# Four of six parts of the modulation as float32 products on TensorE, in groups of 32 columns

## The chip, the cores and the metric

The kernel runs on one core of a Trainium2 chip, in one launch. The metric is the device time in microseconds, the median of several runs. The engines are PE (TensorE, matrix products), DVE (VectorE), ACT (ScalarE), POOL (GpSimd) and SP, whose queue issues the DMAs. Each engine takes its instructions strictly in the order in which they stand in its program.

## The reference

Two layers of a hybrid backbone over 1024 latent tokens of width 1024: a Conformer convolution module and a multi-scale pooling mixer. Each layer is modulated by three vectors of 1024 (shift, scale, gate), products of a vector `silu(c)` with a 1024x3072 matrix. With two layers these are the six parts of the modulation:

```
for i in range(DEPTH):                       # DEPTH = 2, kinds: convolution, pooling
    sh, sc, gt = split((silu(c) @ w_mod[i] + b_mod[i])[:, None, :], 3)
    h = _rms(x, norm_g[i]) * (1.0 + sc) + sh
    o = _conv_mixer(h, ...) if kind == MIX_CONV else _pool_mixer(h, ...)
    x = x + gt * o

def _conv_mixer(h, w_in, dw, db, ln_g, ln_b, w_out):
    a, b, g = split(h @ w_in, 3)
    y = a * sigmoid(b)
    y = depthwise_conv(y, dw, width=31) + db      # along the tokens
    y = silu(_layernorm(y, ln_g, ln_b)) * silu(g)
    return y @ w_out
```

## The kernel before

Channels lie on the 128 partitions in eight tiles (ct or kt from 0 to 7), tokens on the free axis in two halves h of 512. A big product is made of three float32r products (hi x hi, lo x hi, hi x lo) by `mm3` (L192), and the parts hi and lo come from ACT (L156) and from DVE or POOL (L161), for tokens and weights alike.

The order in the program: the first shift and scale (`mod_block`, L300) and `hT`; the first products `pf` for the first half (PSUM names of the products: `pf`, `pg`, `ps` give y, `psg` the gates g); then two parts of the modulation by `gemv` (L262: `gt0`, whose dots run on POOL and ACT, and `sh1` on DVE); the products `pg`; then for the tiles 4 to 7 the products `ps`, with a third part `a1` stepped in between (`step`, L78). Behind the tile 4 stand the convolutions of the tiles 0 to 4 of the first half, and behind each of the next tiles its own. A convolution has 31 taps and runs either on DVE, with accumulators `cv` in PSUM (L448), or on ACT and POOL: ACT scales the shifted tile by a tap into a tile `pr` (L435), and POOL adds it to `z` (L436). POOL has the tiles 1, 3 and 5 of the first half and 1, 3, 5, 6 and 7 of the second. The first layer norm sums the eight `z` (`zsum`, L493), takes the mean on PE (`mu`, L498), the variance (`va`, then `vpz` on PE and `vrz`, a power on POOL, L226) and spreads the result by `rbz` (L231). The gate products `psg` fill PE around it. The output product of the first half, layer 1 for the first half (`psv`, `psq`, `psy`, `psf`) and the convolutions of the second half then run side by side up to the second layer norm. The fourth part, `gt1`, is stepped through layer 1. Behind the second layer norm come the second half's output product and layer 1.

Buffers are rings dealt in the order of the program: `raw` (four buffers) holds raw weights and the rows of `w_mod`, `w` their split parts, `pr` (two buffers) the scaled taps, and the PSUM tag `mm` has five banks. What is dealt later in the program waits until the buffer's last user is done. A scheduler then sets each engine's order; `behind` (L174) and `priority` (L72) steer it.

Of the kernel before, what the change touches and what calls it, by code (L numbers as in the profile page):

```python
# [14 lines left out]
P = 128  # L15
# [42 lines left out]
def hybrid_kernel(ctx, tc, xT, vecs, wm, cv_first, cv_w, cv_wo, pl_w, pl_grp, pl_wo, out):  # L58
# [24 lines left out]
    def unit(tag, name, dt=F32, cols=1024):  # L83
        """A [128, 1024] tile in a ring, or in a slot of a region (a letter and a number)."""
        width = WIDTH.get(tag[0], 1024)
        return S.tile([P, width], dt, tag=tag, name=name, bufs=RINGS.get(tag, 1))[:, :cols]
# [4 lines left out]
    def raw(name):  # L91
        return unit("raw", name)
# [37 lines left out]
    # window / count of the positions whose window is cut by an end of the sequence  # L130
# [17 lines left out]
    nc.vector.tensor_tensor(out=s_c, in0=s_c, in1=VT[:, :, V_C], op=ALU.mult)  # L148
    bsc = const.tile([P, 2, KT], F32, name="bsc")
# [31 lines left out]
    def load_next(out, in_):  # L181
        ordered(nc.sync.dma_start(out=out, in_=in_))
# [17 lines left out]
    def gemm(ps, w, r, after=(), start=KT // 2):  # L200
        """The products from start on are issued behind the instructions given."""
        for kt in range(KT):
            with behind(after if kt >= start else ()):
                mm3(ps, cut(w, bl(kt)), r[kt], kt == 0, kt == KT - 1)

    def diagonals(dg, cols):
        """[128, 4, 128] of the four columns, each on the diagonal of a block."""
        return nc.vector.tensor_tensor(
            out=dg.rearrange("p (j q) -> p j q", j=4),
            in0=ident.unsqueeze(1).broadcast_to((P, 4, P)),  # L210
            in1=cols.unsqueeze(2).broadcast_to((P, 4, P)),
            op=ALU.mult,
        )
# [3 lines left out]
    def rstd_rows(total, name, fill=None):  # L217
        """[128, 512] of 1 / sqrt(sum over the partitions of the total / D + EPS), on every partition."""
# [19 lines left out]
    def squares(xs, name, eng):  # L238
        """A sum of squares over the tiles, which grows by a tile at every call of add."""
        total = half("vs", f"va{name}")  # L240

        def add(i):
            if i == 0:
                nc.scalar.activation(total, xs[i], AF.Square)
                return None
            sq = half("sq", f"sq{name}{i}")
            nc.scalar.activation(sq, xs[i], AF.Square)  # L247
            return eng.tensor_tensor(out=total, in0=total, in1=sq, op=ALU.add)  # L248

        return total, add  # L250

    def dot(w, out, eng):
        """The sum over the rows of w_mod of their product with silu(c), for 128 of the outputs."""
# [8 lines left out]
    def gemv(layer, part, res, eng, after=()):  # L262
        for kt in range(KT):
            w = raw(f"wm{layer}{part}{kt}")
            nc.sync.dma_start(out=w, in_=wm[layer, part, kt])
            with behind(after):
                dot(w, res[:, kt : kt + 1], eng)
            if kt < KT - 1:
                yield True
        add = bsc[:, layer, :] if part == 1 else VT[:, :, V_BM + 3 * layer + part]  # L270
        nc.vector.tensor_tensor(out=res, in0=res, in1=add, op=ALU.add)
        if part == 1:
            nc.vector.tensor_tensor(out=res, in0=res, in1=VT[:, :, V_G0 + layer], op=ALU.mult)

# [17 lines left out]
    s_row = const.tile([P, D], F32, name="s_row")  # L292
# [7 lines left out]
    def mod_block(kt):  # L300
        dots = []
        for part in range(2):
            w = unit("w" if part else "raw", f"wmb{kt}{part}")
            load_next(w, wm[0, part, kt])
# [82 lines left out]
    early = [gemv(0, 2, gt0, nc.gpsimd), gemv(1, 0, sh1, nc.vector)]  # L387
    for i in range(KT):
        with behind(gated if i >= DOTS_AHEAD else []):
            for job in early:  # L390
                next(job, None)
    pending.append(gemv(1, 1, a1, nc.vector))
# [18 lines left out]
    def conv(h, ct, taps=None, count=None):  # L411
        """The convolution of a tile of channels, or the next ones (count) of its taps."""
# [105 lines left out]
    def gate_norm(h, z, rb):  # L518
        """Normed, gated and split; the norm runs two tiles ahead of the rest."""
# [92 lines left out]
    def load_early(part, k):  # L612
        """One of the weights of the first products of layer 1."""
# [120 lines left out]
    def layer1_out(part, ms, ahead=(), last=None, after=(), start=KT // 2):  # L734
        """The output product: of the first ones (ahead, loaded early) a tile of channels per k, the others in turn."""
# [36 lines left out]
    pending.append(gemv(1, 2, gt1, nc.vector))  # L772
# [78 lines left out]
```

## Time and profile before

| | us |
|---|---|
| median of 3 runs | 812.97 |
| lowest, highest | 811.77, 813.42 |
| span of the profiled execution, first to last instruction | 810.0 |
| busy PE, DVE, POOL, ACT in that span | 703.4, 671.5, 566.9, 407.5 |

The runs are device times, the span is the part of one execution that the profiler saw; no other time of that execution is recorded, so what lies around the span is taken as the median less the span, 2.97 us. Matmuls are pipelined and the end of each is modelled, so their spacing, not their length, tells what one costs. An engine that is busy all the time isn't therefore the one on which the end depends; the chain of work and the stretches tell that.

### The profile page before, as it was taken

What the parts mean: (1) busy time and instruction counts of PE and PEld (TensorE: products, weight loads), DVE (VectorE), ACT (ScalarE), POOL (GpSimd) and SP (SyncE); (2) the same over time, 40 slices, a digit from 0 to 9 for tenths busy, and PEclk for the clock granted to TensorE, in tenths of its full rate; (3) what the DMA queues carried; (4) which work ended last, traced back from release to release, by engine and by line L of the source; (5) the groups of instructions that cost most, each with busy time, mean ns of one, the idle gap of its engine ahead of it and who ended that gap; (6) DMA issues with size and microseconds to landing.
All of it is one profiled execution on the core that took longest, in us unless ns stands there. A gap on an engine that the chain in (4) does not pass through costs nothing.

```text
span 810.0 us, 9060 instructions
## 1 busy us (share of the span) xinstructions
PE 703.4 (87%) x3092; PEld 562.2 (69%) x3092; DVE 671.5 (83%) x782; ACT 407.5 (50%) x591; POOL 566.9 (70%) x412
## 2 busy tenths in 40 slices
PE   2887899699999969789899776878799979999998
PEld 1565788488878747468677555656578758888998
DVE  6989999899889799999999899999895572666521
ACT  4543853665666766556766645554332432333210
POOL 3398589999999989789989999898411630444322
PEclk9988999899999989999899978989999989999999
DMA  8673555311012422434521233444642550233232
GB/s 316 239 283 107 189 185 196 104 52 53 27 52 91 168 106 91 144 129 162 179 102 40 78 132 134 137 156 155 233 156 103 158 168 0 91 104 131 79 106 80
DMA packets 36478, 105.63 MB, mean 130 GB/s; under 512 B 4048, under 2 KB 6224, under 8 KB 36432
## 3 DMA queue, kind: packets, MB, share of 16 engines
q1 hardware_dynamic: 36432, 105.05, 37.7%
q8 instruction: 24, 0.39, 0.2%
q14 instruction: 22, 0.18, 0.1%
HBM read 92.45 MB, written 12.58 MB: 130 GB/s over the span
## 4 chain that ended last, share of the span: by engine, by line
DVE 32%; PE 26%; POOL 23%; issue 12%; ACT 4%; DMA 2%; SPq 0%; POOLq 0%; DVEq 0%; ACTq 0%
POOL z L436 18%; DVE cv L448 5%; PE psv L195 2%; PE psv L193 2%; PE psv L194 2%; PE psf L194 2%; PE psf L193 2%; PE psf L195 2%; PE psq L195 2%; PE psq L193 2%; PE psq L194 2%; PE pso L193 2%; PE pso L195 2%; PE pso L194 2%; DVE s L644 2%
## 5 line engine op out<-in xcount | busy, mean ns | idle before, releaser
L436 POOL TENSOR_TENSOR z<-z,pr 128x512 f32<-128x512 f32 (+8 forms) x240 | 381.9, 1592 | 30.7 <-ACT pr L435 16.3
L435 ACT ACTIVATE pr<-y,VT 128x512 f32<-128x512 f32 (+8 forms) x240 | 171.1, 718 | 131.4 <-POOL z L436 128.2
L448 DVE SCALAR_TENSOR_TENSOR cv<-y,VT,cv 128x512 f32<-128x512 f32 (+12 forms) x232 | 160.2, 740 | 0.2
L255 DVE SCALAR_TENSOR_TENSOR wm<-wm,s_row 128x1024 f32<-128x1024 f32 x24 | 44.6, 1861 | 0.1
L640 DVE TENSOR_TENSOR s<-v 128x519 f32<-128x519 f32 (+1 forms) x16 | 21.4, 1341 | 19.5 <-ACT v L689 19.5
L742 DVE SCALAR_TENSOR_TENSOR xf<-psf,gt,xf 128x260 f32<-128x260 f32 (+1 forms) x24 | 13.2, 570 | 29.2 <-PE psf L195 25.2
L259 POOL TENSOR_TENSOR wmb<-wmb,s_row 128x1024 f32<-128x1024 f32 x8 | 22.2, 2772 | 18.2 <-DMA wmb<-in_wm 18.2
L725 DVE SCALAR_TENSOR_TENSOR q<-psy,VT,q 128x260 f32<-128x260 f32 (+1 forms) x24 | 13.5, 569 | 19.2 <-PE psy L195 19.1
L259 POOL TENSOR_TENSOR wm<-wm,s_row 128x1024 f32<-128x1024 f32 x8 | 20.4, 2556 | 12.2 <-DMA wm<-in_wm 12.2
L536 ACT ACTIVATE z<-z,VT 128x512 f32<-128x512 f32 x16 | 12.9, 814 | 27.9 <-DVE z L533 27.9
L644 DVE TENSOR_TENSOR s<-s 128x517 f32<-128x517 f32 (+5 forms) x24 | 22.8, 956 | 0.2
L248 DVE TENSOR_TENSOR vay<-vay,sqy 128x512 f32<-128x512 f32 x14 | 16.5, 1180 | 5.5 <-ACT sqy L247 5.3
L655 DVE SCALAR_TENSOR_TENSOR s<-s,v 128x504 f32<-128x504 f32 (+1 forms) x16 | 19.6, 1235 | 1.4 <-POOL s L653 1.3
L156 ACT CAST y<-q 128x504 fp32r<-128x504 f32 (+1 forms) x16 | 9.9, 616 | 19.7 <-DVE q L725 19.7
L161 DVE TENSOR_TENSOR y<-q,y 128x504 fp32r<-128x504 f32 (+1 forms) x16 | 16.6, 1041 | 3.0 <-ACT y L156 3.0
L161 POOL TENSOR_TENSOR wo16l<-wo,wo16h 128x1024 fp32r<-128x1024 f32 x1 | 2.4, 2393 | 23.5 <-ACT wo16h L156 23.5
L161 DVE TENSOR_TENSOR pd<-s,pd 128x504 fp32r<-128x504 f32 (+1 forms) x16 | 17.5, 1107 | 1.6 <-ACT pd L156 1.4
L255 DVE SCALAR_TENSOR_TENSOR wmb<-wmb,s_row 128x1024 f32<-128x1024 f32 x8 | 15.5, 1933 | 3.0 <-DMA wmb<-in_wm 3.0
L550 DVE SCALAR_TENSOR_TENSOR xr<-pso,gt,xr 128x512 f32<-128x512 f32 x16 | 11.6, 743 | 7.2 <-PE pso L195 7.2
L513 DVE TENSOR_TENSOR va<-va,sqz 128x512 f32<-128x512 f32 x14 | 16.8, 1203 | 0.7
L528 DVE TENSOR_TENSOR z<-z,sgr 128x512 f32<-128x512 f32 x16 | 16.2, 1010 | 1.1 <-ACT z L536 1.1
L156 ACT CAST pd<-s 128x504 fp32r<-128x504 f32 (+1 forms) x16 | 9.7, 617 | 14.5 <-DVE s L655 10.2
(2497 smaller groups left out, 2463.6 us busy)
## 6 DMA issues: line engine op xcount, KB each, us to landing
wm<-in_wm SPq DMA_DIRECT2D x32, 512.0 KB, 3.3
wmb<-in_wm SPq DMA_DIRECT2D x16, 512.0 KB, 6.0
wo<-in_cv_wo SPq DMA_DIRECT2D x16, 512.0 KB, 3.8
wp<-in_pl_wo SPq DMA_DIRECT2D x16, 512.0 KB, 3.2
wg<-in_cv_w SPq DMA_DIRECT2D x12, 512.0 KB, 3.3
wv<-in_pl_w SPq DMA_DIRECT2D x12, 512.0 KB, 3.4
wq<-in_pl_w SPq DMA_DIRECT2D x12, 512.0 KB, 3.3
x<-in_xT SPq DMA_DIRECT2D x16, 256.0 KB, 5.6
```

The lines of the kernel that those rows point to most:

```text
L156: return nc.scalar.copy(hi, src)
L161: return eng.tensor_tensor(out=lo, in0=src, in1=hi.bitcast(F32), op=ALU.subtract)
L193: nc.tensor.matmul(ps, w[0], r[0], start=first, stop=False)
L194: nc.tensor.matmul(ps, w[0], r[1], start=False, stop=False)
L195: nc.tensor.matmul(ps, w[1], r[0], start=False, stop=last)
L255: eng.scalar_tensor_tensor(out=w, in0=w, scalar=1.0, in1=s_row, op0=ALU.mult, op1=ALU.mult, accum_out=out)
L259: eng.tensor_tensor(out=w, in0=w, in1=s_row, op=ALU.mult)
L435: nc.scalar.activation(pr[:, o], y[:, i], AF.Copy, scale=dw(k))
L436: nc.gpsimd.tensor_tensor(out=z[:, o], in0=z[:, o], in1=pr[:, o], op=ALU.add)
L448: nc.vector.scalar_tensor_tensor(out=a[:, o], in0=y[:, i], scalar=dw(k), in1=a[:, o], op0=ALU.mult, op1=ALU.add)
L640: nc.vector.tensor_tensor(out=s[:, :m], in0=v[:, :m], in1=v[:, 1 : m + 1], op=ALU.add)
L644: nc.vector.tensor_tensor(out=s[:, :m], in0=s[:, :m], in1=s[:, step : step + m], op=ALU.add)
```

## The change

The parts `gt0`, `sh1`, `a1` and `gt1` are no longer dots of rows of `w_mod` with a spread `silu(c)` on DVE or POOL. Each half (512 outputs) of a part becomes eight float32 products on PE: the weights are `silu(c)` repeated in 32 columns (`srep`), the data are 512 columns of `w_mod`, and product kt goes to the 32 partitions of group kt mod 4 of one bank `gv`. ACT copies the bank to a tile `row` of the ring `pr`, and four one-column products with a vector `sel`, one at the first partition of each group, add the four groups and turn the row into columns. DVE adds the bias and, for `a1`, multiplies. The bytes loaded are the same, in the same 512 KB pieces through `raw`. The first shift and scale stay as dots. `s_row` moves into a slot of a region, and one `behind` waits for one instruction, not two.

```diff
+    srep = const.tile([P, KT, 32], F32, name="srep")
+    nc.vector.tensor_copy(srep, s_c.unsqueeze(2).broadcast_to((P, KT, 32)))
+    sel = const.tile([P, 1], F32, name="sel")
+    nc.gpsimd.memset(sel, 0.0)
+    for j in range(4):
+        nc.gpsimd.memset(sel[32 * j : 32 * j + 1, :], 1.0)
...
-    def gemv(layer, part, res, eng, after=()):
-        for kt in range(KT):
-            w = raw(f"wm{layer}{part}{kt}")
-            nc.sync.dma_start(out=w, in_=wm[layer, part, kt])
-            with behind(after):
-                dot(w, res[:, kt : kt + 1], eng)
-            if kt < KT - 1:
+    def gemv(job, layer, part, res):
+        for h in range(2):
+            ps = mmps(f"gv{job}{h}")
+            for c in range(4):
+                w = raw(f"wk{job}{h}{c}")
+                nc.sync.dma_start(out=w, in_=wk[job, h, c])
+                for i in range(2):
+                    kt = 2 * c + i
+                    q = slice(32 * (kt % 4), 32 * (kt % 4) + 32)
+                    nc.tensor.matmul(ps[q, :], srep[:, kt, :], w[:, hs(i)], start=kt < 4, stop=kt >= 4)
+                if c < 3:
+                    yield True
+            row = half("pr", f"row{job}{h}")
+            nc.scalar.copy(row[:, :HW], ps)
+            for j in range(4):
+                nc.tensor.matmul(ps[:, j : j + 1], row[:, bl(j)], sel, start=True, stop=True)
+            o = slice(4 * h, 4 * h + 4)
+            add = bsc[:, layer, o] if part == 1 else VT[:, o, V_BM + 3 * layer + part]
+            nc.vector.tensor_tensor(out=res[:, o], in0=ps[:, :4], in1=add, op=ALU.add)
+            if part == 1:
+                nc.vector.tensor_tensor(out=res[:, o], in0=res[:, o], in1=VT[:, o, V_G0 + layer], op=ALU.mult)
+            if h == 0:
                 yield True
...
-    early = [gemv(0, 2, gt0, nc.gpsimd), gemv(1, 0, sh1, nc.vector)]
+    early = [gemv(0, 0, 2, gt0), gemv(1, 1, 0, sh1)]
     for i in range(KT):
-        with behind(gated if i >= DOTS_AHEAD else []):
+        with behind(gated[:1] if i >= DOTS_AHEAD else []):
             for job in early:
                 next(job, None)
-    pending.append(gemv(1, 1, a1, nc.vector))
+    pending.append(gemv(2, 1, 1, a1))
...
-    pending.append(gemv(1, 2, gt1, nc.vector))
+    pending.append(gemv(3, 1, 2, gt1))
```

On ACT, where the first taps of POOL's first convolution are scaled. `pr0114` and `pr010` are the first two taps of tile 1, `sig` the sigmoids of the gates, `row20` the sums of the third part's first half. Before:

```order
L337 ACTIVATE sig20_573<-pf12_179 128x512
L260 ACTIVATE wm021_631,gt0_620<-wm021_631 128x1024
L156 CAST h14h_600<-x12_352 128x512
L337 ACTIVATE sig00_577<-pf10_175 128x512
L432 ACTIVATE z01_1091<-y1_568,VT_66 128x512
L435 ACTIVATE pr0114_1093<-y1_568,VT_66 128x511
L435 ACTIVATE pr010_1096<-y1_568,VT_66 128x497
L156 CAST h14h_600<-x12_352 128x512
```

and in the changed kernel:

```order
L357 ACTIVATE sig31_966<-pg131_916 128x512
L452 ACTIVATE z11_2516<-y1_576,VT_66 128x512
L163 CAST wa4h_986<-wa4_984 128x1024
L452 ACTIVATE z11_2516<-y3_753,VT_66 128x512
L472 ACTIVATE z00_1113<-cv020_1242,VT_66 128x512
L357 ACTIVATE sig40_1057<-ps140_1006 128x512
L284 COPY row20_998<-gv20_975 128x512
L455 ACTIVATE pr0114_1152<-y1_576,VT_66 128x511
L455 ACTIVATE pr010_1155<-y1_576,VT_66 128x497
```

The first tap moved from behind the first gates (`sig00` of `pf`) to behind the sigmoid of `ps140`, the copy `row20` and the end of DVE's convolution of tile 2.

On PE, behind the last products of `pf`. `gv00` and `gv10` are the first halves of the first two parts, `wk` their data. Before:

```order
L195 MATMUL pf00_176<-h06h_501,w07l_520 128x512
L194 MATMUL pf13_181<-h06l_502,w07h_519 128x512
L195 MATMUL pf13_181<-h06h_501,w07l_520 128x512
L193 MATMUL pg030_682<-h00h_199,w00h_195 128x512
L194 MATMUL pg030_682<-h00l_200,w00h_195 128x512
L195 MATMUL pg030_682<-h00h_199,w00l_196 128x512
```

and in the changed kernel:

```order
L280 MATMUL gv00_632<-wk002_650,srep_109 32x512 x2
L280 MATMUL gv10_637<-wk102_654,srep_109 32x512 x2
L280 MATMUL gv00_632<-wk003_658,srep_109 32x512 x2
L286 MATMUL gv00_632<-sel_111,row00_662 128x1 x4
L280 MATMUL gv10_637<-wk103_669,srep_109 32x512 x2
L286 MATMUL gv10_637<-sel_111,row10_673 128x1 x4
L280 MATMUL gv01_680<-wk010_681,srep_109 32x512 x2
L280 MATMUL gv11_685<-wk110_686,srep_109 32x512 x2
L200 MATMUL pg030_728<-h00h_207,w00h_203 128x512
```

Ten loads' products and two reductions came in ahead of the first `pg`; the other six loads of these two parts stand among the `pg`, and the last product of `gv20` stands behind the 24 of `ps140`.

On PE at the first layer norm. `wg30` and `wg50` are weights of the gate products, in the order 0, 2, 1, 3, 4, 6, 5, 7. Before:

```order
L194 MATMUL psg_2082<-h00l,wg30h 128x512
L195 MATMUL psg_2082<-h00h,wg30l 128x512
L193 MATMUL psg_2082<-h00h,wg30h 128x512
L498 MATMUL mu_2240<-zsum_2232,onesd 128x512
L194 MATMUL psg_2082<-h00l,wg30h 128x512
```

and in the changed kernel:

```order
L201 MATMUL psg_2374<-h02l,wg50h 128x512
L202 MATMUL psg_2374<-h02h,wg50l 128x512
L518 MATMUL mu_2310<-zsum_2302,onesd 128x512
L229 MATMUL vpz_2351<-ones,va_2317 128x1 x4
L238 MATMUL rbz_2360<-dgz_2361,ones 128x512
L200 MATMUL psg_2374<-h04h,wg50h 128x512
```

The mean stands 253 rows behind the last `ps`, where it stood 148 behind, and nothing stands between it, the variance and the spread any more. On DVE, around the sums ahead of that mean, before:

```order
L453 TENSOR_TENSOR z03_1480<-z03_1480,cv071_1847 128x512
L493 TENSOR_TENSOR zsum0_2232<-zsum0_2232,z03_1480 128x512
L444 TENSOR_SCALAR cv100_2243<-y0_576,VT_66 128x512
L444 TENSOR_SCALAR cv101_2244<-y0_576,VT_66 128x512
L161 TENSOR_TENSOR wo02l_2229<-wo02_2226,wo02h_2228 128x1024
L161 TENSOR_TENSOR wg40l_2141<-wg40_2138,wg40h_2140 128x1024
L504 TENSOR_TENSOR z00_1054<-z00_1054,mu0_2240 128x512 x2
```

and in the changed kernel:

```order
L168 TENSOR_TENSOR wo02l_2299<-wo02_2296,wo02h_2298 128x1024
L168 TENSOR_TENSOR wg40l_2211<-wg40_2208,wg40h_2210 128x1024
L168 TENSOR_TENSOR wg60l_2245<-wg60_2242,wg60h_2244 128x1024
L168 TENSOR_TENSOR wg50l_2371<-wg50_2368,wg50h_2370 128x1024
L513 TENSOR_TENSOR zsum0_2302<-zsum0_2302,z03_1550 128x512 x2
L464 TENSOR_SCALAR cv100_2313<-y0_584,VT_66 128x512
L464 TENSOR_SCALAR cv101_2314<-y0_584,VT_66 128x512
L168 TENSOR_TENSOR wg70l_2405<-wg70_2402,wg70h_2404 128x1024
L524 TENSOR_TENSOR z00_1113<-z00_1113,mu0_2310 128x512 x2
```

Four splits of weights now stand ahead of the last two sums; before, the first two of them stood behind the sums and the other two among the rows of the variance.

## Rows read from the trace of the kernel before

**Rows 1.** The page: busy us, share and count; the chain's shares by line.

```profile
PE 703.4 (87%) x3092; PEld 562.2 (69%) x3092; DVE 671.5 (83%) x782; ACT 407.5 (50%) x591; POOL 566.9 (70%) x412
POOL z L436 18%; DVE cv L448 5%; PE psv L195 2%; PE psv L193 2%; PE psv L194 2%; PE psf L194 2%; PE psf L193 2%; PE psf L195 2%; PE psq L195 2%; PE psq L193 2%; PE psq L194 2%; PE pso L193 2%; PE pso L195 2%; PE pso L194 2%; DVE s L644 2%
```

**Rows 2.** Stretches: us, busy us and count of each engine, clock, DMA share.

```profile
core 0: us, PE busy (x) PEld busy (x) DVE busy (x) ACT busy (x) POOL busy (x), PEclk, DMA share, GB/s
...
162.20:253.90 91.70, 90.35 (x391) 72.98 (x391) 84.95 (x121) 55.97 (x79) 86.68 (x63) 1.00 0.14 49
...
309.50:559.30 249.80, 210.23 (x836) 161.87 (x835) 245.34 (x255) 153.72 (x223) 227.09 (x161) 0.93 0.36 124
```

**Rows 3.** The same stretch, POOL's additions of L436 alone.

```profile
309.50:559.30 249.80, 198.15 (x120) 0.93 0.36 124
```

**Rows 4.** POOL in order of time: start, us, line, operation; idle before in brackets.

```profile
92.58 3.95 POOL L436 TENSOR_TENSOR z<-z,pr 128x511 f32<-128x511 f32 x2
...
118.49 33.95 POOL L436 TENSOR_TENSOR z<-z,pr 128x502 f32<-128x502 f32 x19
...
309.05 1.02 POOL L226 TENSOR_TENSOR vrz<-vez,mhalf 128x4 f32<-128x4 f32 x1 [1.23 <-DVE vez L224]
...
555.82 1.26 POOL L436 TENSOR_TENSOR z<-z,pr 128x498 f32<-128x498 f32 x1
...
557.63 1.71 POOL L436 TENSOR_TENSOR z<-z,pr 128x497 f32<-128x497 f32 x1
```

**Rows 5.** DVE in order of time, at 82 us and around the first layer norm.

```profile
81.75 1.21 DVE L255 SCALAR_TENSOR_TENSOR wm<-wm,s_row 128x1024 f32<-128x1024 f32 x1
...
276.09 1.21 DVE L161 TENSOR_TENSOR wo02l<-wo,wo02h 128x1024 fp32r<-128x1024 f32 x1
281.56 2.11 DVE L161 TENSOR_TENSOR wg40l<-wg,wg40h 128x1024 fp32r<-128x1024 f32 x1 [4.26 <-ACT wg40h L156]
...
299.16 1.22 DVE L161 TENSOR_TENSOR wg60l<-wg,wg60h 128x1024 fp32r<-128x1024 f32 x1
...
307.27 1.62 DVE L161 TENSOR_TENSOR wg50l<-wg,wg50h 128x1024 fp32r<-128x1024 f32 x1
```

**Rows 6.** PE in order of time: first `pg`, first `ps`, products of float32.

```profile
88.59 0.39 PE L193 MATMUL pg<-h00h,w00h 128*128 128x512 f32 x1
...
138.63 0.39 PE L193 MATMUL ps<-h00h,wb4h 128*128 128x512 f32 x1
...
274.91 1.13 PE L498 MATMUL mu<-zsum,onesd 128*128 128x512 f32 x2 [1.62 <-DVE zsum L493]
275.47 0.80 PE L194 MATMUL psg<-h00l,wg30h 128*128 128x512 f32 x1
276.11 0.40 PE L195 MATMUL psg<-h00h,wg30l 128*128 128x512 f32 x1
...
306.55 0.95 PE L222 MATMUL vpz<-ones,va 128*128 128x1 f32 x8
...
564.41 1.13 PE L498 MATMUL mu<-zsum,onesd 128*128 128x512 f32 x2 [1.15 <-DVE zsum L493]
...
586.87 2.04 PE L231 MATMUL rbz<-dgz,ones 128*128 128x512 f32 x2 [4.30 <-DVE dgz L208]
```

**Rows 7.** Stretches around two of the float32 products, columns as in rows 2.

```profile
274.00:277.00 3.00, 2.09 (x7) 1.43 (x8) 3.00 (x4) 2.38 (x3) 2.84 (x3) 1.00 0.83 257
...
586.80:589.50 2.70, 2.63 (x4) 1.50 (x5) 1.77 (x3) 0.00 (x0) 0.00 (x0) 0.50 0.48 178
```

**Rows 8.** The page: dots and ACT's taps (busy, mean ns, idle before); loads, landing.

```profile
L435 ACT ACTIVATE pr<-y,VT 128x512 f32<-128x512 f32 (+8 forms) x240 | 171.1, 718 | 131.4 <-POOL z L436 128.2
...
L255 DVE SCALAR_TENSOR_TENSOR wm<-wm,s_row 128x1024 f32<-128x1024 f32 x24 | 44.6, 1861 | 0.1
...
L259 POOL TENSOR_TENSOR wm<-wm,s_row 128x1024 f32<-128x1024 f32 x8 | 20.4, 2556 | 12.2 <-DMA wm<-in_wm 12.2
...
wm<-in_wm SPq DMA_DIRECT2D x32, 512.0 KB, 3.3
wmb<-in_wm SPq DMA_DIRECT2D x16, 512.0 KB, 6.0
```

More of the change, by code (lines that the diff above doesn't have):

```diff
@@ L57, in hybrid_kernel @@
 @with_exitstack
-def hybrid_kernel(ctx, tc, xT, vecs, wm, cv_first, cv_w, cv_wo, pl_w, pl_grp, pl_wo, out):
+def hybrid_kernel(ctx, tc, xT, vecs, wm, wk, cv_first, cv_w, cv_wo, pl_w, pl_grp, pl_wo, out):
     nc = tc.nc
@@ L260, in dot @@
             nc.scalar.activation(w, w, AF.Copy, accum_out=out)
-    def gemv(layer, part, res, eng, after=()):
-        for kt in range(KT):
-            w = raw(f"wm{layer}{part}{kt}")
-            nc.sync.dma_start(out=w, in_=wm[layer, part, kt])
-            with behind(after):
-                dot(w, res[:, kt : kt + 1], eng)
-            if kt < KT - 1:
+    def gemv(job, layer, part, res):
[20 more added lines that the diff above has]
+            if h == 0:
                 yield True
[L270 to L273, printed above, removed]
     xs = [None, None]
@@ L290, in hybrid_kernel @@
     sh0 = const.tile([P, KT], F32, name="sh0")
-    s_row = const.tile([P, D], F32, name="s_row")
+    s_row = unit("Y9", "s_row")
     for h in range(2):
@@ L303, in mod_block @@
             w = unit("w" if part else "raw", f"wmb{kt}{part}")
-            load_next(w, wm[0, part, kt])
+            load_next(w, wm[part, kt])
             dots.append(S.tile([P, 1], F32, tag=f"dot{part}", name=f"dot{kt}{part}", bufs=2))
@@ L827 @@
     )
+    wk = np.stack([g["w_mod"][i][:, j * D : (j + 1) * D] for i, j in ((0, 2), (1, 0), (1, 1), (1, 2))])
+    wk = wk.reshape(4, 4, 2, P, 2, HW).transpose(0, 4, 1, 3, 2, 5).reshape(4, 2, 4, P, 1024)
     wf = g["cv_w_in"][0].reshape(KT, P, 3, D)[:, :, :2, : FIRST * P]
@@ L831 @@
         "vecs": vecs,
-        "wm": g["w_mod"].transpose(0, 2, 1).reshape(2, 3, KT, P, D),
+        "wm": g["w_mod"][0].T.reshape(3, KT, P, D)[:2],
+        "wk": wk,
         "cv_first": wf.reshape(KT, P, 2 * FIRST * P),
```

## The prediction

> **What bounds the kernel now.** I read the share of each engine and the chain of work first [rows 1]. No engine stands alone: PE, DVE and POOL are busy for 87, 83 and 70% of the span, and the largest single piece of the chain is POOL's addition of a tap in the convolution, `z` at L436, with 18%. The table by stretches [rows 2] says where: from 162 to 254 us POOL is busy for 86.68 of 91.70 us, and from 309.5 to 559.3 us POOL for 227.09 and DVE for 245.34 of 249.80. Of POOL's time in that second stretch 198.15 us are 120 tap additions [rows 3], 1.65 us each. Up to 560 us the kernel is thus a race between POOL and DVE, and both layer norms wait for the loser. In POOL's own order of time [rows 4] the first two tap additions start at 92.58; four more are done between the dots, and at 118.49 the seventh of 240 begins. The last one ends at 557.63 + 1.71 = 559.34, and the second layer norm's mean on PE starts at 564.41 [rows 6]. From there to the end are 810.0 - 564.4 = 245.6 us, a stage in which PE leads and which the change hardly touches.
>
> **What is removed.** 24 dots on DVE, 44.6 us, and 8 on POOL, 20.4 us plus 12.2 us of waiting for their data [rows 8], with a pass on ACT behind each POOL dot. If PE took the work for nothing, POOL could come to its taps some 26 us sooner (118.49 - 92.58), less six additions at 1.65: about 16 us. This is the whole gain to be had, because POOL's 240 additions stay.
>
> **What is added on PE.** 64 float32 products with 512 columns of data and 32 of weights, and eight reductions of four one-column products. Before has no product on a group of 32 columns. The nearest row is the float32 product of the mean, 128 columns wide: it starts at 274.91, and the second product behind it at 276.11; with 0.23 us for the one between, it took 1.20 - 0.23 = 0.97 us [rows 6] at a granted clock of 1.00 [rows 7], the upper level (2.4 GHz). At the lower level (granted clock 0.50, 1.2 GHz) the product at 586.87 took 2.04 us. Bounds: a quarter of 0.97 (four groups at once) and 2.04; I take 0.97, the row nearest in kind. A reduction is the row at 306.55: 0.95 us. A product of the gemms takes (138.63 - 88.59) / 216 = 0.232 us [rows 6].
>
> **What is moved, and this decides.** Each half of a part now copies its sums into a `row` tile of the ring `pr`, which has two buffers and also carries every scaled tap from ACT to POOL. The ring is dealt in program order, and the first half of the third part (`row20`) is asked for before the first convolution. In ACT's order the first tap product, `pr0114`, therefore stands behind `row20<-gv20`. That copy needs the last product of `gv20` on PE, which stands behind all `pg` products and all of `ps140`. So POOL stands still until PE is there. Worked out:
>
> 1. PE reaches the first added product at 88.59 - 1.14 = 87.45: the DVE dot at 81.75, which stood ahead of `h06l`, is gone [rows 5, 6].
> 2. From there to the last product of `gv20` PE's order has 242 gemm products, 242 x 0.232 = 56.1; 40 added ones, 40 x 0.97 = 38.8; four reductions, 4 x 0.95 = 3.8; the first two of these follow their ACT copy at once, 2 x 0.72 by the ACT pass of the same size [rows 8], 1.4. Sum 187.5. The data come along: a buffer of the four is free for some 5.8 us (three others at 1.94) and a load lands in 3.3 to 6.0 [rows 8]; if they took longer, ten loads in a row would each add the difference. The copy and the first tap product add 1.4: POOL starts at about 189.
> 3. POOL then has 94 instructions up to its last tile of the first half, at 91.70 / 63 = 1.456 each [rows 2] 136.9: it is done at 326. The mean of the first layer norm, however, now stands on PE behind nearly all fill products: 610 gemm products (141.3), eight added ones (7.8) and two reductions (1.9) after `gv20`, so at 187.5 + 151.0 = 338.5. PE is the later. Before it was 274.91: **+64**.
> 4. From the mean to the power on POOL (`vrz`) it was 309.05 - 274.91 = 34.1 us. In it DVE did `wo02l` 1.21, a wait of 4.26, `wg40l` 2.11, `wg60l` 1.22 and `wg50l` 1.62 [rows 5]; all of them now stand ahead of the mean, and `wg70l` comes in, for which I take 1.4: 34.1 - 10.4 + 1.4 = 25.1. The power is at 363.6, **+55**. The fill that covered this time on PE is used up, so PE idles there.
> 5. After the power POOL had 120 tap additions and took 559.34 - 309.05 = 250.3. Now only 16 additions of the next tile, not 30, stand ahead of it, so 14 more follow: 14 x 1.65 = 23.1. Against this stand POOL's 22.7 us of idle time in that stretch (249.80 - 227.09), waits for DVE and ACT which a later POOL meets less often, and eight dots that no longer press on it. Between 0 and -22.7 I take -15. The last addition ends at 363.6 + 258.4 = 622.0: **+62.7**. DVE has 245.3 - 8 x 1.86 = 230 us of work for these 258, so it doesn't take the lead.
> 6. The fourth part's two reductions stand ahead of the second mean and wait for the ring until POOL is done: + 1.9. Held banks of PSUM cost PE nothing that the chain sees, since it waits for POOL there. The tail of 245.6 stays.
>
> Span 810.0 + 62.7 + 1.9 = 874.6. The median of the runs lies 812.97 - 810.0 = 2.97 above the profiled span; with it the time is **877.6 us**. The copies and tiny additions on DVE (16 of 128x4 and the like) lie in its new idle time; were DVE still full they would cost some 3 us.
>
> **A page that speaks against the change.** The Trainium skill, page TensorEngine Tiling (Array Packing), section Tiling Modes, says that going from one tiling mode to another drains TensorE. No row of before shows such a change. By that rule, each of some 50 changes between full and 32-column products could lose the 0.16 us by which a product's 0.39 us exceeds its 0.232 (an estimate), some 8 us more at most.
>
> **Rivals.**
> - *Groups overlap.* Two products on different groups run side by side, so a load's two products take 0.97 and not 1.94. In the first ten loads the data then set the pace, (0.97 + 3.3 to 6.0) / 4, about 1.4 us a load: 5.4 saved; 9.7 in the next ten and 3.9 in the four before the mean. That gives 877.6 - 19.0 = 858.6. For it: the two write to different partitions of a bank; against it: no row shows two products at once. The Trainium skill, page TensorE: Matmul & The Clock Gate, section Part 3: Packing small matmuls, reports 2.38 times for three column groups; this is the rule of this rival, and no run here shows it so far.
> - *Lower clock.* At 587 the granted clock was 0.50, behind a wait of PE of 4.30 us [rows 6, 7]; PE waits here too, for the ACT copies and for data. If the 20 products that stand together run at the lower level, 20 x (2.04 - 0.97) = 21.4 is added: 899.0; if all 48 up to the mean do, 929.0.
> - *POOL catches up* (the other side). With DVE less full, every addition after the power takes the shortest row, 1.26 us at 555.82 [rows 4], and POOL never waits: 134 x 1.26 + 28.9 of its other work (227.09 - 198.15) = 197.7. POOL is done at 561.3, and the time is about 817. It turns to faster than before at 1.23 us an addition, or when the groups overlap as well: 798. Against it: DVE still has 230 us of work in these 258, and at 98% DVE the mean was 1.65.
>
> **How the numbers follow.** Forecast 0.52 (862 to 893). Groups overlap 0.25 (848 to 866). Lower clock 0.12 (890 to 930). POOL catches up in part, still slower, 0.07 (815 to 848). It does so wholly, faster, 0.03; within 0.2% (about 1.6 us, what a measurement of this kernel can tell from no change) 0.01. Slower is 0.96. The range from 845 to 905 takes the forecast, the overlap and the lower half of the clock case, some 0.82.
>
> **What would show it.** POOL idle from about 77 to 189 us, its first `z` addition right behind the ACT copy of `row20`; spacing of the added products 0.97 (or 0.5, or 2.04) us; the first mean near 338 with `vpz` and `rbz` behind it and PE idle between them; the last `z` near 622; the tail 246. I'm wrong if POOL starts before 150, or if its additions fall to 1.3 us.

## The result, and the profile after

The changed kernel takes 867.57 us (median of 4 runs, 863.29 to 871.26) against 813.05 us of the kernel before in the same comparison: a ratio of 1.066, 95% interval 1.062 to 1.070. It is slower by some 55 us. Its profiled execution has a span of 869.4 us, 59.4 more than the 810.0 of before; that execution took 871.26 us, 3.7 more than the median. The line numbers below are those of the changed kernel: the tap addition `z` is L456, ACT's scaling `pr` L455, the added products `gv` L280, the copy `row` L284, the reductions L286, the first and second mean `mu` L518.

The page of the changed kernel, engines and the chain's shares by line, which answer to [rows 1]:

```profile
PE 742.9 (85%) x3284; PEld 574.8 (66%) x3284; DVE 620.2 (71%) x740; ACT 404.6 (47%) x583; POOL 523.7 (60%) x409
POOL z L456 12%; DVE cv L468 4%; PE ps L200 2%; PE ps L202 2%; PE ps L201 2%; PE gv L280 2%; PE psv L200 2%; PE psv L202 2%; PE psv L201 2%; PE psf L200 2%; PE psf L201 2%; PE psf L202 2%; PE pg L201 2%; PE pg L200 2%; PE pg L202 2%
```

DVE lost 51 us of work and POOL 43, PE gained 40. All three fill a smaller share of the longer span than before, PE 85% (87 before), DVE 71 (83) and POOL 60 (70): the time went into waiting. POOL's own order of time (start, us, line, operation, idle before in brackets), as [rows 4]:

```profile
69.17 7.98 POOL L346 TENSOR_TENSOR x<-x,rbs 128x512 f32<-128x512 f32 x4 [2.49 <-ACT rbs L395]
173.52 1.28 POOL L456 TENSOR_TENSOR z<-z,pr 128x511 f32<-128x511 f32 x1 [96.38 <-ACT pr L455]
...
348.57 1.02 POOL L233 TENSOR_TENSOR vrz<-vez,mhalf 128x4 f32<-128x4 f32 x1 [3.48 <-DVE vez L231]
...
596.19 17.12 POOL L456 TENSOR_TENSOR z<-z,pr 128x509 f32<-128x509 f32 x13 [1.13 <-ACT pr L455]
```

POOL stands still for 96.38 us and begins its 240 additions at 173.52, where before began at 92.58. ACT at that moment shows what it waited for:

```profile
170.84 0.60 ACT L357 ACTIVATE sig<-ps 128x512 f32<-128x512 f32 x1 [5.08 <-PE ps L202]
172.24 0.58 ACT L284 COPY row<-gv 128x512 f32<-128x512 f32 x1 [0.80 <-PE gv L280]
172.72 0.73 ACT L455 ACTIVATE pr<-y,VT 128x511 f32<-128x511 f32 x1
```

The first tap product `pr` comes right behind `row<-gv` (`row20`), and that waited for PE. PE in order of time, with the first added products, a load's two products among `pg`, the two layer norms, and the reductions of the fourth part, as [rows 6]:

```profile
83.05 1.93 PE L280 MATMUL gv<-wk,srep 128*32 128x512 f32 x16
...
107.19 0.39 PE L201 MATMUL pg<-h04l,w04h 128*128 128x512 f32 x1
107.51 1.05 PE L280 MATMUL gv<-wk,srep 128*32 128x512 f32 x4
108.49 0.49 PE L202 MATMUL pg<-h04h,w04l 128*128 128x512 f32 x1
...
322.50 1.12 PE L518 MATMUL mu<-zsum,onesd 128*128 128x512 f32 x2 [0.81 <-DVE zsum L513]
346.43 1.87 PE L229 MATMUL vpz<-ones,va 128*128 128x1 f32 x8 [22.80 <-DVE va L533]
351.51 2.04 PE L238 MATMUL rbz<-dgz,ones 128*128 128x512 f32 x2 [3.22 <-DVE dgz L215]
...
612.67 3.57 PE L286 MATMUL gv<-sel,row 128*128 128x1 f32 x16 [16.83 <-ACT row L284]
...
620.72 1.02 PE L518 MATMUL mu<-zsum,onesd 128*128 128x512 f32 x2
```

A float32 product has two records, so `x4` is a load's two products. Behind the first mean PE is idle for 22.80 us, since its fill is used up. The stretches (us, then busy us and count of PE, PEld, DVE, ACT, POOL, then granted clock, DMA share and GB/s), as [rows 2]:

```profile
104.00:172.20 68.20, 68.20 (x301) 48.29 (x299) 40.28 (x62) 9.74 (x14) 0.00 (x0) 1.00 0.28 100
172.20:322.50 150.30, 146.94 (x642) 116.15 (x643) 101.18 (x131) 93.32 (x133) 136.17 (x97) 1.00 0.29 97
...
348.50:614.00 265.50, 214.21 (x849) 159.00 (x849) 229.24 (x238) 165.17 (x239) 235.76 (x176) 0.90 0.35 115
```

From 104 to 322.5 PE hardly pauses, and POOL stands still for the first 69 us of it. Before, PE was as full in that part (90.35 of 91.70 us from 162 to 254 [rows 2]), but POOL and DVE were full beside it. Of the last stretch, the tap additions alone, as [rows 3]:

```profile
348.50:614.00 265.50, 207.36 (x134) 0.90 0.35 115
```

That is 1.55 us each, against 1.65 before, but 134 of them and not 120.

The milestones of all kernels below, in us of their profiled executions, with the median of their runs. "Taps" is POOL's first and last addition, "mean" and "power" those of the two layer norms.

| kernel | first tap | mean 1 | power 1 | last tap ends | mean 2 | power 2 | span | median |
|---|---|---|---|---|---|---|---|---|
| before | 92.6 | 274.9 | 309.1 | 559.3 | 564.4 | 582.8 | 810.0 | 813.1 |
| after | 173.5 | 322.5 | 348.6 | 613.3 | 620.7 | 640.4 | 869.4 | 867.6 |
| ring_only | 148.7 | 294.6 | 320.2 | 592.5 | 596.7 | 611.3 | 839.4 | 839.9 |
| own_ring | 87.5 | 288.3 | 322.6 | 539.9 | 545.2 | 584.3 | 812.6 | 813.3 |
| row20_in | 174.4 | 323.5 | 349.5 | 613.7 | 618.0 | 632.6 | 861.3 | 857.6 |
| row20_out | 124.8 | 290.4 | 320.4 | 554.4 | 559.6 | 597.9 | 825.1 | 827.0 |
| one_group | 180.5 | 326.7 | 356.5 | 619.4 | 627.7 | 647.9 | 874.9 | 877.8 |
| gt1_alone | 94.6 | 275.6 | 309.7 | 554.1 | 558.9 | 579.2 | 806.6 | 807.4 |
| late_gt1_a1 | 93.8 | 268.0 | 302.9 | 541.7 | 548.2 | 575.9 | 804.6 | 806.3 |
| late_all | 86.2 | 266.7 | 299.6 | 513.8 | 537.3 | 583.3 | 810.8 | 812.6 |
| late_all_free | 85.6 | 263.3 | 296.8 | 513.0 | 537.0 | 569.4 | 810.3 | 810.9 |

### The profile page after: what moved, and what is told of

Same layout as the page of the kernel before. It is cut to its first block, busy times and chain, and to the rows that moved or that the text cites. A ratio compares the mean times of both kernels' runs of the same rounds, so it can differ in the third digit from the quotient of the medians.

```text
span 869.4 us, 9393 instructions
## 1 busy us (share of the span) xinstructions
PE 742.9 (85%) x3284; PEld 574.8 (66%) x3284; DVE 620.2 (71%) x740; ACT 404.6 (47%) x583; POOL 523.7 (60%) x409
## 4 chain that ended last, share of the span: by engine, by line
PE 41%; DVE 23%; POOL 17%; issue 10%; DMA 4%; ACT 4%; SPq 0%; POOLq 0%; DVEq 0%; ACTq 0%
POOL z L456 12%; DVE cv L468 4%; PE ps L200 2%; PE ps L202 2%; PE ps L201 2%; PE gv L280 2%; PE psv L200 2%; PE psv L202 2%; PE psv L201 2%; PE psf L200 2%; PE psf L201 2%; PE psf L202 2%; PE pg L201 2%; PE pg L200 2%; PE pg L202 2%
## 5 line engine op out<-in xcount | busy, mean ns | idle before, releaser
L456 POOL TENSOR_TENSOR z<-z,pr 128x512 f32<-128x512 f32 (+8 forms) x240 | 360.0, 1500 | 133.0 <-ACT pr L455 119.7
L455 ACT ACTIVATE pr<-y,VT 128x512 f32<-128x512 f32 (+8 forms) x240 | 170.8, 718 | 121.1 <-POOL z L456 119.6
L468 DVE SCALAR_TENSOR_TENSOR cv<-y,VT,cv 128x512 f32<-128x512 f32 (+15 forms) x232 | 159.0, 742 | 0.3
L280 PE MATMUL gv<-wk,srep 128*32 128x512 f32 x128 | 30.1, 644 | 5.6 <-DMA wk<-in_wk 5.6
L762 DVE SCALAR_TENSOR_TENSOR xf<-psf,gt,xf 128x260 f32<-128x260 f32 (+1 forms) x24 | 13.2, 570 | 30.3 <-PE psf L202 24.9
L286 PE MATMUL gv<-sel,row 128*128 128x1 f32 x64 | 11.0, 298 | 18.2 <-ACT row L284 18.2
L286 PEld LDWEIGHTS gv<-sel,row 128*128 128x128 f32 x64 | 11.1, 260 | 21.8 <-ACT row L284 21.6
L229 PE MATMUL vpz<-ones,va 128*128 128x1 f32 x16 | 2.8, 297 | 22.8 <-DVE va L533 22.8
L229 PEld LDWEIGHTS vpz<-ones,va 128*128 128x128 f32 x16 | 2.8, 260 | 23.7 <-DVE va L533 23.6
```

The source lines that it names most:

```text
L280: nc.tensor.matmul(ps[q, :], srep[:, kt, :], w[:, hs(i)], start=kt < 4, stop=kt >= 4)
L286: nc.tensor.matmul(ps[:, j : j + 1], row[:, bl(j)], sel, start=True, stop=True)
L455: nc.scalar.activation(pr[:, o], y[:, i], AF.Copy, scale=dw(k))
L456: nc.gpsimd.tensor_tensor(out=z[:, o], in0=z[:, o], in1=pr[:, o], op=ALU.add)
L468: nc.vector.scalar_tensor_tensor(out=a[:, o], in0=y[:, i], scalar=dw(k), in1=a[:, o], op0=ALU.mult, op1=ALU.add)
```

## Experiments: the ring and the products, one without the other

**The products without the shared ring (own_ring).**

```diff
-    RINGS = {..., "pr": 2, "vs": 1}
+    RINGS = {..., "pr": 2, "vs": 1, "rw": 1}
-            row = half("pr", f"row{job}{h}")
+            row = half("rw", f"row{job}{h}")
```

> The changed kernel with one edit: the tile `row` has a ring of its own (one buffer) and no longer shares `pr` with the scaled taps. Theory (the ring holds POOL back): POOL's first tap addition starts before 115 us instead of 173.5, the mean of the first layer norm stands on PE at row 949 and not 1023, so (74 x 0.232 = 17 us fewer products ahead of it, some of PE's waits gone) it starts at 290 to 305 instead of 322.5, the fill stands behind it again, 120 and not 134 additions follow the power: about 823 us (810 to 835), still slower than before because PE's added products are now what the first mean waits for. Rival (the added products themselves make the kernel slow, the ring matters little): above 855 us. Second rival (PE has room for them): 800 to 810 us, faster than before.

Measured: 813.28 us, ratio 1.001 (0.999 to 1.003). It is as fast as before, so all of the 55 us are gone with one name changed. POOL begins at 87.47:

```profile
87.47 2.59 POOL L456 TENSOR_TENSOR z<-z,pr 128x511 f32<-128x511 f32 x2 [10.36 <-ACT pr L455]
```

The first mean, at 288.31, is 2 us ahead of the expected range (290 to 305). The time is 10 us better than the 823 expected, inside its range: POOL was further when the later mean came, only 109 additions follow the power, and the last ends at 539.9, 19 us ahead of before. The forecast "still slower than before" was thus wrong for this kernel; the second rival, that PE has room, overstated it. The 19 us are lost again before the second power, which stands at 584.3 (582.8 before). The stretch from the last addition to that power, before and then in own_ring, columns as above:

```profile
559.40:582.80 23.40, 19.81 (x84) 14.59 (x82) 21.17 (x26) 7.53 (x12) 12.36 (x5) 1.00 0.70 245
```

```profile
540.00:584.20 44.20, 43.31 (x197) 33.77 (x195) 30.00 (x39) 18.18 (x25) 18.91 (x11) 1.00 0.72 236
```

PE has more than twice the products there and hardly pauses.

**The ring without the products (ring_only).** In the kernel before:

```diff
                 gemm(ps[n, h], w, hT[h])
+                if (ct, h, n) == (FIRST, 0, 1):
+                    row = half("pr", "rowx")
+                    nc.scalar.copy(row[:, :HW], ps[n, h])
```

> The kernel before with one edit: behind the products `ps140` ACT copies their bank into a tile of the ring `pr`, which nobody reads. No product on PE is added, and all dots stay. Theory (the ring holds POOL back): ACT's first tap product stands behind that copy, POOL begins its taps at about 146 us and not at 92.6, the first mean stands on PE at row 1027 with variance and spread right behind it, at about 303 us instead of 274.9 (+28), the last addition about 34 us later: 847 us (835 to 858). Rival (the added float32 products are the cause): 813 us, as before.

Measured: 839.91 us, ratio 1.033 (1.031 to 1.035): one copy of 0.59 us, read by nobody, costs 27 us. ACT and then POOL in this kernel (L435 and L436 as in the kernel before):

```profile
146.95 0.59 ACT L467 COPY rowx<-ps 128x512 f32<-128x512 f32 x1 [1.09 <-PE ps L195]
147.43 0.60 ACT L337 ACTIVATE sig<-ps 128x512 f32<-128x512 f32 x1
147.92 1.32 ACT L435 ACTIVATE pr<-y,VT 128x511 f32<-128x511 f32 x2
```

```profile
111.25 2.39 POOL L259 TENSOR_TENSOR wm<-wm,s_row 128x1024 f32<-128x1024 f32 x1 [2.41 <-DMA wm<-in_wm]
148.72 3.99 POOL L436 TENSOR_TENSOR z<-z,pr 128x511 f32<-128x511 f32 x3 [35.08 <-ACT pr L435]
```

The picture is that of the changed kernel: the first tap product behind the copy, and behind the first mean PE idle for 22.43 us. The mean came at 294.58, 8 us earlier than expected:

```profile
294.58 1.02 PE L501 MATMUL mu<-zsum,onesd 128*128 128x512 f32 x2
318.04 1.87 PE L222 MATMUL vpz<-ones,va 128*128 128x1 f32 x8 [22.43 <-DVE va L516]
```

So the ring alone costs 27 us, the products together with the dots that they save nothing, and both changes 55. The rest is an interaction: the ring ties POOL to a point on PE, the end of `ps140` and `gv20`, and the added products move that point from 147 to 172 us. The first mean moves with it, from 294.6 to 322.5.

## Experiments: which of the eight rows

```diff
-            row = half("pr", f"row{job}{h}")
+            row = half("sq" if (job, h) == (2, 0) else "pr", f"row{job}{h}")   # row20_out
+            row = half("pr" if (job, h) == (2, 0) else "sq", f"row{job}{h}")   # row20_in
```

> The changed kernel with one edit: only the copy `row20`, the first half of the third part, goes to another ring (`sq`); the other seven rows stay in `pr`. Theory (the one row asked for between the early products and the first convolution does the harm): POOL waits only for the rows of the early parts, whose last copy was at about 124 us, so its first tap addition starts at 100 to 126 us and not at 173.5; the first mean starts at 288 to 295 us; 813 to 825 us. Rival (all eight rows share the harm evenly): one eighth of the 54 us comes back, some 860 us.

> The counterpart of the run with `row20` out: seven of the eight rows of the changed kernel go to another ring (`sq`), and only `row20`, the first half of the third part, stays in `pr`. Theory (this one row makes POOL wait for PE): POOL's first tap addition at about 172 us, the first mean at about 322 us, 862 to 870 us, as the changed kernel. Rival (the rows of the early parts and of the fourth part have a share of more than 10 us): below 858 us.

Measured: 826.99 us (ratio 1.018, 1.016 to 1.020) with `row20` out, 857.59 us (1.057, 1.053 to 1.061) with `row20` alone in `pr`. The first POOL addition of each kernel, row20_out and then row20_in:

```profile
124.76 5.34 POOL L456 TENSOR_TENSOR z<-z,pr 128x511 f32<-128x511 f32 x4 [47.27 <-ACT pr L455]
```

```profile
174.40 1.28 POOL L456 TENSOR_TENSOR z<-z,pr 128x511 f32<-128x511 f32 x1 [96.80 <-ACT pr L455]
```

One row of eight makes the whole of the first wait, as the theory had it. The first and second parts' rows hold POOL to 124.8 when `row20` is out. The time of row20_out is 2 us over its range, though first tap and first mean are in theirs: its second power follows the mean by 38.3 us, where before needed 18.4. And row20_in, 10 us below the changed kernel, lies just inside its rival's range (below 858), not in the theory's, although first tap, first mean and last tap of the two agree within about 1 us. The other seven rows do have a share, and it lies behind the last tap. In row20_in PE reads:

```profile
617.95 1.13 PE L518 MATMUL mu<-zsum,onesd 128*128 128x512 f32 x2 [1.95 <-DVE zsum L513]
630.49 1.87 PE L229 MATMUL vpz<-ones,va 128*128 128x1 f32 x8 [11.42 <-DVE va L533]
```

The rows of the fourth part no longer wait for POOL's last taps, so PE does not stand for 16.83 us in front of the reductions at 612.67, and the products of layer 1 that stood behind them are done earlier. The second power follows its mean by 14.7 us instead of 19.6; in all, the two profiled executions differ by 8.1 us.

## Experiment: the groups

```diff
-                    nc.tensor.matmul(ps[q, :], srep[:, kt, :], w[:, hs(i)], start=kt < 4, stop=kt >= 4)
+                    nc.tensor.matmul(ps[:32, :], srep[:, kt, :], w[:, hs(i)], start=kt == 0, stop=kt == KT - 1)
...
-                nc.tensor.matmul(ps[:, j : j + 1], row[:, bl(j)], sel, start=True, stop=True)
+                nc.tensor.matmul(ps[:, j : j + 1], row[:32, bl(j)], sel[:32, :], start=True, stop=True)
```

> The changed kernel with one edit: all eight products of a half go to the same group of 32 columns, one sum over eight, and the reductions have 32 partitions. As many products, no two of them side by side. Theory (groups run side by side, and the ring makes POOL wait for PE): two products of a load take about 1.75 us and not 0.9 in the rows, so each load ahead of the first mean adds up to 0.85 us: 24 loads, some of them hidden behind waits for data: the first tap addition of POOL about 12 us later than 173.5, the first mean 14 to 20 us later than 322.5, 880 us (875 to 890). Rival (products on different groups don't overlap, or PE isn't on the path): 868 us, as the changed kernel.

Measured: 877.83 us, ratio to before 1.079 (1.077 to 1.082). The total is as expected. Three loads in a row, and a load's two products among `pg`, in this kernel (`gv` is L279 here):

```profile
103.62 5.34 PE L279 MATMUL gv<-wk,srep 128*32 128x512 f32 x12
108.89 0.50 PE L201 MATMUL pg<-h00l,w01h 128*128 128x512 f32 x1
...
110.85 0.39 PE L200 MATMUL pg<-h04h,w04h 128*128 128x512 f32 x1
111.16 1.90 PE L279 MATMUL gv<-wk,srep 128*32 128x512 f32 x4
113.00 0.50 PE L201 MATMUL pg<-h04l,w04h 128*128 128x512 f32 x1
```

From the `pg` ahead to the `pg` behind it is 2.15 us here, 1.30 in the changed kernel. Less 0.23 for one full product, two float32 products cost 1.92 one after the other and 1.07 side by side on two groups. That the groups overlap is shown. The Trainium skill, page TensorE: Matmul & The Clock Gate, section Part 3: Packing small matmuls, reports such concurrency, and the trace agrees: 1.8 times for two groups.

The 0.96 each without overlap is the price that the prediction took from the mean's product (0.97), and it includes what the visit among full products costs. From the first one's start to the next `pg`, six products take 5.27 us and two take 1.84 (111.16 to 113.00), so each further product costs 0.86, and the visit adds 1.92 - 2 x 0.86 = 0.20 us. Side by side, 1.07 is one product and the visit: the second product costs nothing. The Trainium skill, page TensorEngine Tiling (Array Packing), section Tiling Modes, says that a change of tiling mode drains TensorE; here the two changes of a visit cost 0.20 us together, 0.10 a change, where the prediction's estimate was 0.16.

The places were not as expected. POOL starts 7 us later and not 12, the first mean comes only 4 us later and not 14 to 20, since PE had waits there for data that the slower products filled: one_group is without any from 83 to 180.5 us. Between `gv20` and the mean its order has fewer products besides (617 records of PE, 642 in the changed kernel). In the profiled executions the sum is 5.5 us, in the medians 10: the profiled execution of the changed kernel lies 3.7 us above its median, that of one_group 1.1 below.

## Experiments: what the offload is worth with the ring out of the way

In these kernels `row` lies in the ring `sq`, the weights are a broadcast of silu(c) without the tile `srep`, `s_row` keeps its place as a constant, and the parts not named stay dots on their engines. For `gt1` alone:

```diff
-    early = [gemv(0, 0, 2, gt0), gemv(1, 1, 0, sh1)]
+    early = [dots(0, 2, gt0, nc.gpsimd), dots(1, 0, sh1, nc.vector)]
...
-    pending.append(gemv(2, 1, 1, a1))
+    pending.append(dots(1, 1, a1, nc.vector))
```

The next three put `gemv(0, ...)` or `gemv(1, ...)` or both back. The late ones take `sh1` or `a1` out of their places and ask for them behind the first layer norm:

```diff
+    pending += [gemv(1, 1, 0, sh1), gemv(2, 1, 1, a1)]   # late_gt1_a1: the second alone
+    step(100)
     y1, done = gate_norm(0, z, rb)
```

> Only the fourth part `gt1` as products on PE, its `row` in the ring `sq`, the weights a broadcast of silu(c) instead of the tile `srep`; the other three parts are dots as before. Theory (where DVE was the fuller engine, taking work from it gains; the ring and the early products were the loss): the first mean stays near 275 us, DVE sheds 8 x 1.86 = 14.9 us in the stretch from the first power to the last addition, in which PE has 40 us free; POOL's additions get shorter or wait less: 803 us (797 to 811). Rival (POOL alone sets that stretch): 811 to 815 us. Rival (products among others always cost): above 816 us.

> As the kernel with `gt1` alone on PE, and `gt0` on PE too (its rows in the ring `sq` as well), so that POOL loses its eight dots; `sh1` and `a1` stay dots on DVE. Theory (a part gains only where the engine that it frees is the late one, and PE's room is some two parts): the first mean stays near 275 us, since DVE sets it, POOL is some 15 us further by then, the last addition comes at 540 to 552 us instead of 554; the second spread on PE is at 578 to 584: 800 to 807 us. Rival (PE is the bound of the second norm already): 808 to 813 us.

> As the kernel with `gt1` alone on PE, and `sh1` on PE too (rows in the ring `sq`); `gt0` stays on POOL, `a1` on DVE. Theory: DVE sheds 8 x 1.86 = 14.9 us ahead of the first mean, PE takes some 7 us more ahead of it and had 11 us of waits there; the first mean at 268 to 275 us, the time 800 to 808 us. Rival (PE is late at the first mean as with all four parts): first mean at 280 us, time 810 to 815 us.

> As the kernel with `gt1` alone on PE, with `gt0` and `sh1` on PE as well (rows in the ring `sq`); only `a1` stays on DVE. Theory (PE's room is some two parts): the first mean is set by PE at about 281 us, between 275.6 with one part and 288.3 with four; POOL is earlier at its end, but the second spread on PE is at 584 to 588: 807 to 813 us. Rival (each part that leaves DVE or POOL gains): below 802 us.

> `gt1` and `a1` on PE, rows in the ring `sq`, and all of `a1` asked for behind the first layer norm, where PE waits between the output products; no added product stands ahead of the first mean. `gt0` and `sh1` stay dots. Theory (what counts is PE's work ahead of the first mean): DVE sheds 14.9 us ahead of it, PE takes nothing more; PE had about 8 us of waits there, so the first mean is at 266 to 272 us and not at 275.6, the second spread some 3 to 7 us earlier than with `gt1` alone: 800 to 806 us. Rival (PE's whole work sets the end): 809 to 814 us.

> All four parts on PE, rows in the ring `sq`; `sh1` and `a1` are asked for behind the first layer norm, only `gt0` stands ahead of it (DVE has no dots of them, POOL neither). Theory (PE's work ahead of the first mean counts): the first mean at 268 to 277 us, where own_ring had 288.3; the time 802 to 809 us. Rival (PE's whole work sets the end): 811 to 817 us, as own_ring.

| parts on PE | median | ratio to before, 95% interval |
|---|---|---|
| `gt1` (gt1_alone) | 807.37 | 0.993 (0.991 to 0.994) |
| `gt1`, `gt0` | 809.03 | 0.995 (0.993 to 0.997) |
| `gt1`, `sh1` | 816.79 | 1.006 (1.004 to 1.007) |
| `gt1`, `gt0`, `sh1` | 817.04 | 1.004 (1.002 to 1.007) |
| `gt1`, `a1` late (late_gt1_a1) | 806.33 | 0.993 (0.991 to 0.996) |
| all, two late (late_all) | 812.60 | 1.000 (0.999 to 1.002) |

Three of these are below the kernel before with their whole interval: `gt1` alone and `gt1` with a late `a1`, each by 0.7%, and `gt1` with `gt0`, by 0.5%. Only the first two are near what the theory gave, at its slower end. `gt1_gt0` and `late_all` came out by their rivals. With `sh1` on PE the first mean came at 283 to 284 us, not at 275 or 281, and both such kernels were slower than either of their expectations. In `gt1_sh1` PE waited 8.7 us for the data of its first products (3.23, 1.95 and 3.47 us), about as much as that mean is late; but in `gt1_gt0_sh1` these waits are 2.8 us and the mean is no earlier, so they aren't shown to be the cause. Why neither kernel gains I can't say.

The late kernels did move what they should. In late_gt1_a1 the first mean stands at 268.03, and in late_all POOL's last addition (L465 here) starts at 512.24, 45 us ahead of before:

```profile
512.24 1.59 POOL L465 TENSOR_TENSOR z<-z,pr 128x497 f32<-128x497 f32 x1
513.91 1.62 POOL L522 TENSOR_TENSOR zsum<-zsum,z 128x512 f32<-128x512 f32 x1
```

Yet its second power comes at 583.34, where it was before. DVE in that time (L533 subtracts the mean here), and then the stretch from the last addition to the second power, columns as above:

```profile
550.52 0.15 DVE L299 TENSOR_TENSOR gt<-gv,VT 128x4 f32<-128x4 f32 x1
562.41 0.74 DVE L756 SCALAR_TENSOR_TENSOR q<-psy,VT,q 128x504 f32<-128x504 f32 x1 [11.74 <-PE psy L200]
563.89 0.69 DVE L166 TENSOR_TENSOR y<-q,y 128x504 fp32r<-128x504 f32 x1 [0.74 <-ACT y L161]
569.06 0.74 DVE L756 SCALAR_TENSOR_TENSOR q<-psy,VT,q 128x504 f32<-128x504 f32 x1 [4.49 <-PE psy L200]
569.72 1.27 DVE L533 TENSOR_TENSOR z<-z,mu 128x512 f32<-128x512 f32 x2
```

```profile
513.90:583.30 69.40, 67.98 (x306) 52.58 (x304) 46.12 (x66) 26.37 (x36) 20.22 (x17) 1.00 0.64 220
```

DVE's subtractions of the mean stand behind `q<-psy`, the mixing of layer 1's first half, and that waits for PE, which is busy for 67.98 of 69.40 us. The last run takes this order away:

```diff
-        z, rb, rb_done = layernorm(1, None, mixed)
+        z, rb, rb_done = layernorm(1)
```

> As the kernel with all four parts on PE and two of them late, and the second layer norm no longer held behind the mixing products of layer 1's first half (the third argument of `layernorm(1, None, mixed)` is left out). In the run before, POOL had its last addition at 513.8 us, but the second power came only at 583.3, since DVE's subtractions of the mean stood behind `q<-psy` and that behind PE. Theory (PE's whole work sets the end by now): the power comes earlier, but the products of layer 1 that stood ahead of it follow later; what can be gained is PE's wait around the second norm, some 5 us of 812.6: 804 to 811 us. Rival (the hold ahead of the second norm is the bound): the tail of some 227 us behind the power follows it, 780 to 797 us.

Measured: 810.87 us, ratio 0.998 (0.997 to 1.000). The second power comes at 569.4, 14 us earlier, and 13 of these are given back: from the power to the end it is 240.9 us, where all the other kernels of the table need 227 to 229. So it was not the hold: the products that stood ahead of the power stand behind it now. From the power to the end PE is busy for 231.65 of 240.9 us with 1213 records, in late_all for 212.93 of 227.5 us with 1131. This is the theory's account, that PE's own work sets the end: it is busy for 732.4 us in own_ring and in this kernel (90%), 29 us more than before, and behind the last tap what DVE and POOL save can't come out. That PE bounds the whole kernel isn't shown: from the first power to the last tap it still stands for 24.9 of 214.6 us, and no run tried to fill these.

## Why the prediction was right, and where its sizes were off

The time was forecast as 877.6 us and is 867.6: slower as said, inside the forecast's own range, and by the mechanism said, POOL held back by the ring until PE is there. One condition of the forecast was wrong, that the products don't overlap. The rival that had them overlap gave 858.6, 9.0 us too little, where the forecast is 10.0 too much. That the time lies in the forecast's range (862 to 893) and not in that rival's (848 to 866) is luck: the errors of steps 5 and 6 have the other sign. The steps in order:

1. **First added product.** 87.45 forecast, 83.05 measured; the end of the `pf` products came 4.4 us earlier than the removed dot alone explained.
2. **The wait of POOL.** First tap right behind `row20`, as forecast, at 173.5 and not 189; 4.4 us of this are those of step 1. The mis-sized term is the 40 added products, 38.8 us. From 83.05 to 172.19 are 89.1 us; without 56.1 for the gemm products, 7.0 of waits (2.48 + 0.47 + 2.68 for data, 0.68 + 0.69 for ACT) and 5.4 for the four reductions, 20.6 us are left, 0.52 each. The rival "groups overlap" had this term nearly right: 23.7 with the waits for data, against 26.2 measured.
3. **The first mean, set by PE.** From `gv20` on 151.0 us forecast and 150.3 measured; it stands at 322.5, not 338.5, by the errors of steps 1 and 2. It did wait 0.81 us for DVE, whose sums stood behind the split of `wg50`, which answers to [rows 5]:

```profile
316.93 2.12 DVE L168 TENSOR_TENSOR wg50l<-wg,wg50h 128x1024 fp32r<-128x1024 f32 x1 [4.25 <-ACT wg50h L163]
318.97 3.47 DVE L513 TENSOR_TENSOR zsum<-zsum,z 128x512 f32<-128x512 f32 x2
```

4. **Mean to power.** 25.1 forecast, 26.1 measured, with PE idle in between as said.
5. **POOL's rest.** 258.4 us forecast for 134 additions, 264.7 measured. I had taken 15 us off for fewer waits. The additions did get shorter, 1.55 instead of 1.65, but POOL's idle time in the stretch rose from 22.7 to 29.7 us. This step was 6 us too small, and hid part of the error of step 2.
6. **The fourth part and the tail.** From the last tap to the second mean 7.4 us, 7.0 forecast. But that holding PE there costs "nothing that the chain sees" was wrong: PE stood for 16.83 us in front of the two reductions, with products of layer 1 behind them. The tail is 248.7 us and not 245.6, and with these rows elsewhere (row20_in) 243.4; the two medians differ by 10 us.

Against the span of 874.6 the steps give -15.0 up to the first power, +6.3 for POOL, +0.4 and +3.1 behind it: 869.4. The overlap rival had taken off 19.0 us where the first steps gave 15.0, and had none of the other three. These make 5.2 of the 10.0 us by which the forecast is off. The other 4.8 are no step: the median lies 1.8 us below the profiled span, where the forecast put it 2.97 above.

The largest wrong belief shows only in the experiments. I put the gain to be had at 16 us, by POOL's earlier start. With the ring out of the way POOL starts earlier and ends 19 us earlier (own_ring), and the time doesn't change, because PE, which that account left out, is the next bound behind the last tap. A row that I read for POOL alone showed how full PE was: 90.35 of 91.70 us [rows 2]. The rival "lower clock" came true in a small way: the granted clock fell to 0.55, mostly the lower level (1.2 GHz), between 92.6 and 104 us, behind three waits for data, and in one_group, where PE had none of these waits, it stayed at 1.00:

```profile
83.00:92.60 9.60, 4.08 (x25) 0.71 (x24) 7.04 (x12) 5.86 (x11) 0.00 (x0) 1.00 0.77 250
92.60:104.00 11.40, 9.93 (x32) 4.43 (x32) 5.02 (x10) 1.17 (x2) 0.00 (x0) 0.55 0.47 162
```

```profile
83.00:100.00 17.00, 17.00 (x46) 4.97 (x46) 14.44 (x24) 6.93 (x13) 0.00 (x0) 1.00 0.68 235
```

## What to carry to other kernels

A buffer ring that is dealt in program order ties all its users together: before a small tile goes into a ring, see which engine its writer waits for and who is dealt the next buffer. Here one copy of 0.6 us in the wrong ring cost 27 us by itself and 55 with the products that moved its release. And before work is taken from the engine that is late, read how full the next one is: with the ring mended, four parts on PE gained nothing, one part, or two with the second one late, 0.7%.

## What the runs showed of the hardware

At a granted clock of 1.00, float32 products of 32 columns on different groups ran fully side by side. In the changed kernel the sixteen records at 83.05 us start four at a time, the fours 0.43 to 0.45 us apart, which is the distance of single records in one_group: four groups for the price of one. Among full products two took 1.07 us instead of 1.92, and the visit by itself some 0.20 us. PE's granted clock fell to 0.55 between 92.6 and 104 us, after waits of 0.5 to 2.7 us for data at 85 to 93 us.
